# A hybrid RWKV-7 layer on one core: all SBUF buffers begin at the same remainder modulo 256 bytes

## The chip, the core and the metric

The kernel runs on one core of one Trainium2 chip. The metric is the device time of one execution in microseconds; lower is better. Everything is float32; most matrix products read their operands as float32r.

## The reference

One decoder layer (DEPTH 1) on x [1, 2048, 1024]: RWKV-7 time mixing, then a gated MLP with a causal depthwise convolution of width 3, each followed by a residual and a LayerNorm.

```
xx = shift(x) - x;  xr, xw, xk, xv, xa, xg = (x + xx * mix[i] for i in range(6))
r, k, v = xr @ w_rkv[0], xk @ w_rkv[1], xv @ w_rkv[2]          # 1024 x 1024 each
decay, a, gate = three two-layer LoRAs (64, 64 and 160 wide)
for each token t and head (16 heads of 64):                    # the recurrence
    state = state * w_t + (state . -kk_t) (kk_t * a_t) + v_t k_t;  y_t = state . r_t
x = LayerNorm(alpha * x + ((head_norm(y) + bonus) * gate) @ w_o)
h = causal_conv3(x @ w_in) + b;  u, g = split(h)               # 1024 -> 5632
x = LayerNorm(alpha * x + (silu(g) * u) @ w_out)               # 2816 -> 1024
```

## The kernel before

The program has four phases. **Sweeps** (about 9 to 715 us): three passes over the tokens, for k, r and v in this order. A pass takes 8 groups of 256 tokens; a group makes two token tiles of 128 by two halves `h` of 512 columns, and each of these four has 24 matmuls into one PSUM tile `ps`. **The recurrence** (to about 1280 us): 16 tiles of 128 tokens, in chunks of 64, by many small float32 products. **The output projection** (`z`, to about 1490 us). **The gated MLP** (to about 2965 us): four blocks of 512 tokens; in each, 22 chunks of 128 hidden units make two runs of 24 matmuls into `ps` (8 slices of the contraction, three products each) and, one chunk behind, 12 matmuls into the output accumulators `acc` for the first 512 columns. After the chunks the second 512 columns follow, all `acc`.

Every float32 product of these kinds is made of three float32r products (`mm3`, lines 139 to 143): both operands are split into a high and a low part by ACT and DVE, and TensorE multiplies high by high, low by high and high by low. So each of these matmuls loads its own 128x128 weights and then streams 512 columns. In the rows of the trace a matmul reads `out<-moving,weights`: `ps<-xH,wiH` streams xH over the weights wiH.

The order of the instructions is made by `Plan`, a list scheduler with a duration and a priority for each group. It reads nothing of addresses, and each engine then runs its list in order.

SBUF tiles come from pools (`tc.tile_pool`). A pool has a number of slots for each tag; a stack of pools grows upward from the left end of memory (`side="left"`), another downward from the right end (`side="right"`). The first tile on the left is `ident`, 512 bytes of each partition at address 16512; the right end is address 229344. Sizes that are no multiple of 256 bytes (`hb` with 514 floats, `xT` with 8 x 257, the small statistics tiles) move all that lies beyond them.

Of the kernel before, what the change touches and what calls it, by code (L numbers as in the profile page):

```python
# [11 lines left out]
F32 = mybir.dt.float32  # L12
# [5 lines left out]
PSUM = bass.MemoryType.PSUM  # L18
DRAM = bass.MemoryType.DRAM
# [11 lines left out]
def bc_rows(ap, n=128):  # L31
    """A DRAM row [1, n] read by every partition."""
    return bass.AP(tensor=ap.tensor, offset=ap.offset, ap=[[0, n], [1, ap.shape[-1]]])

# [5 lines left out]
class Plan:  # L40
    """Issue order of a set of instruction groups: each group runs on one engine, may take slots of a pool when it
    starts and give slots back when it ends; engines take the most urgent group that is ready. With fifo (or for
    the pools in it), the groups take the slots of a pool in the order in which they were added."""
# [74 lines left out]
class K:  # L118
# [3 lines left out]

    def ld(self, out, in_):
        return self.nc.sync.dma_start(out, in_)

    st = ld
# [7 lines left out]
    def split(self, H, L, x):  # L134
        """x = H + L exactly enough for float32: each part carries 12 bits."""
        self.nc.scalar.activation(H, x, AF.Copy)
        self.nc.vector.tensor_tensor(L, x, H, op=OP.subtract)
# [7 lines left out]
    def rsqrt(self, pool, out, x, n, m=None):  # L145
        """out = x ** -0.5 elementwise, [128, n], by Newton from a bit guess."""
        nc = self.nc
        w = pool.tile([128, n], F32, name="rsw", bufs=1)[:, 0:m or n]
        y = pool.tile([128, n], F32, name="rsy", bufs=1)[:, 0:m or n]
        nc.vector.tensor_scalar(w.bitcast(I32), x.bitcast(I32), 1, None, op0=OP.arith_shift_right)  # L150
        nc.vector.tensor_scalar(y.bitcast(I32), w.bitcast(I32), -1.0, float(0x5F3759DF), op0=OP.mult, op1=OP.add)
        for i in range(3):
            nc.vector.tensor_tensor(w, y, y, op=OP.mult)
            nc.vector.scalar_tensor_tensor(w, w, -0.5, x, op0=OP.mult, op1=OP.mult)
            nc.vector.scalar_tensor_tensor(out if i == 2 else y, w, 1.5, y, op0=OP.add, op1=OP.mult)

    # ------------------------------------------------------------------ run
    def run(self, phases="ASWF", scratch=None):
        tc, nc, a = self.tc, self.nc, self.a
        with ExitStack() as ctx:  # L160
# [3 lines left out]
            for t in range(NT):  # L164
                for q in ("vc", "Y"):
                    self.S[q, t] = mk([128, D], f"{q}_{t}")
                self.S["gs", t] = mk([128, 2, D], f"gs_{t}")
                for h in range(2):
                    # row t + 1 holds token t, but for the key, which is one row ahead, with the first token's last too
                    s = mk([129, 5, 512], f"in_{t}_{h}")  # L170
                    self.S["in", t, h] = s[1:129]
                    for i, q in enumerate(("r", "kp", "kkn", "b", "th")):
                        self.S[q, t, h] = s[0:128, i] if q == "kkn" else s[1:129, i]
                    self.S["kk0", t, h] = s[128:129, 2]
                    c = slice(h * 512, h * 512 + 512)
                    for q in ("vc", "Y"):
                        self.S[q, t, h] = self.S[q, t][:, c]
                    self.S["gateg", t, h] = self.S["gs", t][:, 0, c]
                    self.S["svbg", t, h] = self.S["gs", t][:, 1, c]
# [5 lines left out]
            self.ident = top.tile([128, 128], F32, name="ident")  # L185
# [17 lines left out]
    # -------------------------------------------------- projections, LoRAs  # L203
# [3 lines left out]
    def a_nodes(self, ctx, pl):  # L207
        """Adds the groups; returns those which end with part of the memory free, and all of it."""
# [4 lines left out]
        E = lambda **kw: st2.enter_context(tc.tile_pool(reuse_waits="tile", **kw))  # L213
# [7 lines left out]
        # what the recurrence's first tile can have before the end  # L221
        E = lambda **kw: st1.enter_context(tc.tile_pool(reuse_waits="tile", side="right", **kw))
# [41 lines left out]
        for sw, (q, wi, mm, ml) in enumerate((("k", 1, 2, 4), ("r", 0, 0, 1), ("v", 2, 3, 5))):  # L264
# [13 lines left out]
            def two(prio, ref, n_ld, d, fH, fL, deps=(), take=()):  # L278
                """ACT then DVE on a staged tile"""
                n1 = pl.add("ACT", 0.52 * d, prio, fH, [n_ld] + list(deps), take=take)  # L280
                return pl.add("DVE", 0.6 * d, prio, fL, [n1], give=("stg",))

            # first layer of the LoRA
# [27 lines left out]
            # the projection  # L311
# [16 lines left out]
            # what starts first: the first sweep with the projection, the others with the LoRA  # L328
# [7 lines left out]
            # second layer of the LoRA  # L336
# [59 lines left out]
            users = []  # L396
# [4 lines left out]
            def front(g):  # L401
# [4 lines left out]
                # the very first products go by parts of the contraction, and before the LoRA's  # L406
# [54 lines left out]
                # hidden units of the LoRA  # L461
                pn = prep("l", ml, wt + o["l0"] if start else gb + o["ml"], ("xT",) if start else ())

                def f_l1(X=X, sw=sw, q=q):
                    """The hidden units of the LoRA, in two parts that are added later."""
                    hp = X["hp"] = ph.tile([128, 256], F32, name="hp")
                    A = C["l1A", sw]
                    for k in range(KD):
# [4 lines left out]
                        else:  # L473
                            # the even and the odd parts in the two halves of the columns
# [57 lines left out]
            # the first halves of the last groups come before the second ones, for the next sweep's weights  # L532
# [196 lines left out]
    # ------------------------------------------------------ the recurrence  # L729
# [4 lines left out]
    def s_nodes(self, ctx, pl, n_1, n_2, w, f):  # L734
        """Adds the groups; n_1 frees part of the memory, n_2 all of it."""
# [3 lines left out]
        Q = {}  # L739
# [10 lines left out]
        def f_open1():  # L750
            """On the right, what W and the FFN have first at the top."""
            nonlocal inv, wkp, ldp, pw, xui, triI, gmask, cols, gm4, nbI, nbIn, nbE, scE
            E = lambda st=pools1, **kw: st.enter_context(tc.tile_pool(reuse_waits="tile", side="right", **kw))
# [13 lines left out]
            # one head's rows of a pair, zeros in the other's: the products use all rows of the array  # L767
# [3 lines left out]
        def f_open2():  # L771
            nonlocal cst, wk, ch2, sm, pm, pc
            E = lambda st=pools2, **kw: st.enter_context(tc.tile_pool(reuse_waits="tile", side="left", **kw))
# [39 lines left out]
        for t in range(NT):  # L813
# [4 lines left out]
            for h in range(2):  # L818
# [54 lines left out]
                for i, n_x in ((0, n_M), (1, n_R)):  # L873
# [7 lines left out]
                    def f_ar(t=t, h=h, i=i):  # L881
# [3 lines left out]
                        else:  # L885
                            # row t holds the key of the token after it, the last row that of the first
# [50 lines left out]
            # the inverses  # L937
# [45 lines left out]
            for c in range(2):  # L983
# [11 lines left out]
                # the block above them  # L995
# [35 lines left out]
                def f_ga(t=t, c=c):  # L1031
                    # A_ab has been read: its columns take the decayed keys, next to A_ak
                    for e in range(2):
                        CP(V[t]["Gm"][es(e), e, c, :, 0:64], V[t]["AR"][es(e), c, :, 0])
# [7 lines left out]
            # the chunks in turn  # L1042
# [7 lines left out]
            # a chunk's step; that of the last tiles in halves of the heads, which follow one another closely  # L1050
# [94 lines left out]
        # products into a spare bank where the engine would fall to its slow clock  # L1145
# [13 lines left out]
    # ------------------------------------ output projection, first LayerNorm  # L1159
# [4 lines left out]
    def w_nodes(self, ctx, pl, n_first, n_ch1, xds, Q, n_rest, stores, f):  # L1164
        """Adds the groups to the recurrence's plan; n_first frees part of its memory, n_ch1 the pool ch1 in Q, n_rest the rest."""
# [11 lines left out]
        def f_open(early):  # L1177
            E = lambda st=ctx, **kw: st.enter_context(
                tc.tile_pool(reuse_waits="tile", side="right" if early else "left", **kw))
# [16 lines left out]
        def f_ch1():  # L1196
            """What the first two tiles need before the recurrence ends."""
# [18 lines left out]
        def weights(h, k):  # L1216
            i = 8 * h + k

            def f_ld():
                # the high and low parts take what the recurrence has left  # L1220
# [45 lines left out]
        def rsqrt(t, u, pr, deps):  # L1266
            """One rsqrt: the heads' norms of tile t, the LayerNorm's of tile u."""
# [32 lines left out]
        def bank(kind, early):  # L1300
            """The PSUM banks in turn, the early ones alone before the recurrence ends."""
# [56 lines left out]
        for t in range(NT):  # L1358
# [4 lines left out]
            for h in range(2):  # L1363
                e = bank("pz", t < 1)
                if t < 2:
                    # in small groups, as the weights come, between the recurrence's last
# [54 lines left out]
    # --------------------------------------------------- gated MLP with conv  # L1421
# [3 lines left out]
    def f_nodes(self, ctx, pl, Q, n_early, n_w, n_rest, zs, gn, n_sx, n_x1):  # L1425
        """Adds the groups to the plan; n_early, n_w and n_rest free more and more memory."""
# [18 lines left out]
        def f_mid():  # L1445
            E = lambda **kw: ctx.enter_context(tc.tile_pool(reuse_waits="tile", side="right", **kw))
# [4 lines left out]
        def f_rest():  # L1451
            E = lambda **kw: ctx.enter_context(tc.tile_pool(reuse_waits="tile", side="left", **kw))
# [27 lines left out]
        xfree = []          # the last users of the x tiles of the block before  # L1480
        for B in range(NB):
# [29 lines left out]
            # the banks of the first products and of the outputs' first half change places from block to block  # L1511
# [10 lines left out]
            def wout(f, h, pr, mm=True, acc_mm=acc_mm, abank=abank, an=an, accs=accs):  # L1522
                """One chunk's part of the outputs; returns the last groups of the token tiles, or the weights."""
# [111 lines left out]
            def add(h, tl, n, pr, XR=XR, accs=accs, LN=LN, xrn=xrn, abank=abank):  # L1635
                """The residual and the statistics of half a row."""
# [49 lines left out]
            # the last chunks' weights stay, and the token tiles end one after another  # L1686
# [96 lines left out]
```

## Time and profile before

| | |
|---|---|
| runs, us | 2981.27, 2984.16, 2985.99 (median 2984.16) |
| span of the profiled execution, us | 2981.2 |
| TensorE matmul busy, share | 2845.6 us, 95% |
| VectorE busy, share | 2084.5 us, 70% |
| ScalarE busy, share | 1740.4 us, 58% |
| DMA packets, bytes | 298555, 424.08 MB |

The profiled execution's own time is its span: 2981.2 us, 3.0 us under the median of the runs. Matmuls overlap their neighbours in the trace, so the mean length of one in a row (some 396 ns) is not its share of the time. What one costs is the distance from its start to the start of the next: the start of the first of a run is taken from the start of what follows the run, and divided by the count.

### The profile page before, as it was taken

Reading aid. Unit: us, or ns where it says so; the run is one execution under the profiler, and the core shown is the slowest. Engines: PE = TensorE matmul, PEld = TensorE weight load, DVE = VectorE, ACT = ScalarE, POOL = GpSimd, SP = SyncE. Lnnn points to the kernel's source line nnn. Section 1 sums busy time; section 2 is a strip of 40 time slices with the busy share of each in tenths; the row PEclk is TensorE's granted clock in tenths of the full one; section 3 lists DMA queues with packets and bytes.
Section 4 is the critical chain, followed back from the end, with each engine's and each line's share of the span. In section 5 each row is a group of like instructions: output and inputs, shape, how many; then the busy total and the mean of one; then the engine's idle time right before and its main releaser. Section 6 shows DMA issues by size and latency. Waiting matters only on the chain.

```text
span 2981.2 us, 51766 instructions
## 1 busy us (share of the span) xinstructions
PE 2845.6 (95%) x19392; PEld 2321.1 (78%) x19392; DVE 2084.5 (70%) x4288; ACT 1740.4 (58%) x4668; POOL 53.6 (2%) x96
## 2 busy tenths in 40 slices
PE   7999999998799999799999999999999999999997
PEld 5776778887677777678888887888888888888886
DVE  7888768986899999779765555474554745547454
ACT  8888557664578788878454444444444444444441
POOL 0000000001000000001100000000000000000000
PEclk9999999999899999799999999999999999999999
DMA  6346555435455565568552223242232422324222
GB/s 202 143 167 222 175 183 191 152 114 175 129 149 161 153 164 160 133 220 315 179 178 94 92 97 120 93 154 97 89 127 96 148 98 85 133 95 153 90 87 78
DMA packets 298555, 424.08 MB, mean 142 GB/s; under 512 B 153952, under 2 KB 179552, under 8 KB 294208
## 3 DMA queue, kind: packets, MB, share of 16 engines
q1 hardware_dynamic: 286976, 379.87, 39.5%
q0 software_dynamic: 11328, 40.90, 3.8%
q8 instruction: 153, 2.51, 0.4%
q14 instruction: 98, 0.80, 0.1%
HBM read 311.57 MB, written 109.12 MB: 141 GB/s over the span
## 4 chain that ended last, share of the span: by engine, by line
issue 56%; PE 20%; DVE 12%; ACT 8%; DMA 3%; POOL 1%; SPq 0%; POOLq 0%; ACTq 0%; DVEq 0%
PE ps L141 4%; PE ps L142 4%; PE ps L143 4%; DVE BKn L904 3%; ACT junk L619 3%; PE G L744 2%; DVE itmp L966 1%; DVE XU L971 1%; DVE Gm L931 1%; PE Y L744 1%; DMA l<-in 1%; ACT junk L1260 1%; PE csI L744 1%; ACT UV L743 1%; PE tb L912 1%
## 5 line engine op out<-in xcount | busy, mean ns | idle before, releaser
L143 PE MATMUL ps<-xH,wiL 128*128 128x512 f32 x1408 | 557.9, 396 | 0.5 <-DVE wiL L1571 0.3
L1571 DVE TENSOR_TENSOR wiL<-wis,wiH 128x1024 fp32r<-128x1024 f32 x176 | 215.4, 1224 | 488.5 <-ACT wiH L1432 488.5
L141 PE MATMUL ps<-xH,wiH 128*128 128x512 f32 x1408 | 556.9, 396 | 0.0
L142 PE MATMUL ps<-xL,wiH 128*128 128x512 f32 x1408 | 556.8, 395 | 0.0
L1432 ACT ACTIVATE hb<-ps 128x512 f32<-128x512 f32 x176 | 105.3, 598 | 518.9 <-PE ps L143 518.8
L141 PE MATMUL ps<-WH,xiH 128*128 128x512 f32 x768 | 307.5, 400 | 14.6 <-ACT xiH L231 9.1
L143 PEld LDWEIGHTS ps<-xH,wiL 128*128 128x128 f32 x1408 | 264.5, 188 | 65.6 <-DVE wiL L1571 2.1
L142 PEld LDWEIGHTS ps<-xL,wiH 128*128 128x128 f32 x1408 | 264.4, 188 | 63.7
L141 PEld LDWEIGHTS ps<-xH,wiH 128*128 128x128 f32 x1408 | 264.5, 188 | 62.9
L142 PE MATMUL ps<-WL,xiH 128*128 128x512 f32 x768 | 305.1, 397 | 2.0 <-DVE WL L326 2.0
L143 PE MATMUL ps<-WH,xiL 128*128 128x512 f32 x768 | 304.4, 396 | 0.0
L1599 DVE SCALAR_TENSOR_TENSOR cv<-hb,cw,cv 128x512 f32<-128x512 f32 x352 | 263.4, 748 | 20.7 <-ACT cv L1595 14.5
L142 PE MATMUL acc<-woL,aH 128*128 128x512 f32 x688 | 269.3, 391 | 1.5 <-DVE woL L1536 1.5
L143 PE MATMUL acc<-woH,aL 128*128 128x512 f32 x688 | 269.9, 392 | 0.0
L141 PE MATMUL acc<-woH,aH 128*128 128x512 f32 x688 | 268.5, 390 | 0.0
L1432 ACT ACTIVATE wiH<-wis 128x1024 fp32r<-128x1024 f32 x178 | 188.8, 1061 | 5.8 <-DMA wis<-in_w_in_dram 5.8
L141 PEld LDWEIGHTS ps<-WH,xiH 128*128 128x128 f32 x768 | 146.3, 190 | 54.4 <-ACT xiH L231 9.1
L1432 ACT ACTIVATE woH<-wos 128x512 fp32r<-128x512 f32 x172 | 108.7, 633 | 114.4 <-PE acc L143 110.1
L142 PEld LDWEIGHTS ps<-WL,xiH 128*128 128x128 f32 x768 | 146.5, 191 | 34.6 <-DVE WL L326 2.5
L143 PEld LDWEIGHTS ps<-WH,xiL 128*128 128x128 f32 x768 | 146.3, 190 | 33.5 <-DVE xiL L450 0.2
L142 PEld LDWEIGHTS acc<-woL,aH 128*128 128x128 f32 x688 | 129.2, 188 | 32.4 <-DVE woL L1536 3.1
L141 PEld LDWEIGHTS acc<-woH,aH 128*128 128x128 f32 x688 | 129.2, 188 | 29.1 <-ACT woH L1432 0.5
(243 smaller groups left out, 5351.8 us busy)
## 6 DMA issues: line engine op xcount, KB each, us to landing
wis<-in_w_in_dram SPq DMA_DIRECT2D x176, 512.0 KB
wos<-in_w_out_dram SPq DMA_DIRECT2D x172, 256.0 KB
l<-in SPq DMA_DIRECT2D x32, 1280.0 KB
xT<-in_xT_dram SPq DMA_DIRECT2D x21, 1028.0 KB
in<-kp SPq DMA_DIRECT2D x64, 256.0 KB
stg<-in_w_rkv_dram SPq DMA_DIRECT2D x48, 256.0 KB
gs<-gs SPq DMA_DIRECT2D x24, 512.0 KB
in<-kr SPq DMA_DIRECT2D x32, 256.0 KB
```

The source lines that it names most:

```text
L141: nc.tensor.matmul(ps, lH, rH, start=start, stop=False)
L142: nc.tensor.matmul(ps, lH, rL, start=False, stop=False)
L143: nc.tensor.matmul(ps, lL, rH, start=False, stop=stop)
L619: nc.scalar.activation(junk, Z["kr"][:, 64 * i:64 * i + 64], AF.Square, accum_out=st["ss"][:, tl, i:i + 1])
L743: CP = lambda out, in_, **kw: nc.scalar.activation(out, in_, AF.Copy, **kw)
L744: MM = lambda out, l, r, **kw: nc.tensor.matmul(out, l, r, **{**dict(start=True, stop=True), **kw}, skip_group_check=True)
L904: TT(dst[rows, :, e], pe8(l[:, 1 if part else 3], e), pe8(V[t]["Pi", h], e), op=OP.mult)
L912: nc.tensor.transpose(ps[:, p], V[t]["BKn"][:, c, hd:hd + 2].rearrange("q e i -> q (e i)"), self.ident)
L931: TT(V[t]["Gm"][:, e, c, 4 * h:4 * h + 4], V[t]["G", h, c, e], gm4, op=OP.mult)
L1432: CP = lambda out, in_, **kw: nc.scalar.activation(out, in_, AF.Copy, **kw)
L1571: TT(W["L"], W["s"], W["H"], op=OP.subtract)
L1599: STT(R[j], W["hb"][:, i:i + 512], C["cw"][:, fc, i:i + 1], R[j], op0=OP.mult, op1=OP.add)
```

## The change: one remainder for all SBUF buffers

SBUF pools are wrapped in `Pool256`. Its `tile` pads the free size of a tile so that all slots of a tag together take a multiple of 256 bytes; what the kernel then uses is the unpadded part. `ident` is padded by 24 floats at its front (608 bytes in place of 512), which moves the left stack from remainder 128 to 224, the remainder of the right end. PSUM and DRAM pools stay as they were.

```
+class Pool256:
+    def tile(self, shape, dtype, bufs=None, **kw):
+        b = bufs or self.bufs
+        n = math.prod(shape[1:])
+        u = 64 // math.gcd(64, 16 * b) * 16 if n % 64 else 64
+        if n % u == 0 or n % 64 == 0:
+            return self.pool.tile(shape, dtype, bufs=b, **kw)
+        x = self.pool.tile([shape[0], -(-n // u) * u], dtype, bufs=b, **kw)[:, 0:n]
...
+    def pool(self, st, **kw):
+        p = st.enter_context(self.tc.tile_pool(**kw))
+        return p if kw.get("space") is not None else Pool256(p, kw["bufs"])
...
-            self.ident = top.tile([128, 128], F32, name="ident")
+            self.ident = top.tile([128, 152], F32, name="ident")[:, 24:152]
...
-        E = lambda **kw: st2.enter_context(tc.tile_pool(reuse_waits="tile", **kw))
+        E = lambda **kw: self.pool(st2, reuse_waits="tile", **kw)
```

The last edit is made for each stack of pools. The diff also drops comments and docstrings, which moves line numbers and makes no instruction. Every engine has the same instructions in the same order as before, on the same slots; a few waits of the first sweep on GpSimd's memsets are held by a neighbouring instruction. What differs is the addresses. The remainder modulo 256 at which the operands of the large products begin, in the two built programs (slices into a tile go by multiples of 512 bytes):

| product (moving, weights) | matmuls | before | after |
|---|---|---|---|
| MLP `ps` (xH or xL, wiH or wiL) | 4224 | 128, 160 | 224, 224 |
| MLP `acc`, chunks 0 to 9 (woH or woL, aH or aL) | 960 | 224, 224 | 224, 224 |
| MLP `acc`, chunks 10 to 21 (48 more, of other tiles, went from 160, 160) | 1104 | 224, 160 | 224, 224 |
| sweeps `ps`, first half h=0 (WH or WL, xiH or xiL) | 1152 | 224, 0 | 224, 224 |
| sweeps `ps`, second half h=1 | 1152 | 0, 0 | 224, 224 |
| `z` (wo, woH or woL, with yH or yL) | 672 | 160, 160 | 224, 224 |
| `z` (the same, with yE of the first two tiles) | 96 | 160, 128 | 224, 224 |

The tiles from which the sweeps store (`kp`, `kr`, `w`, `av`) go from remainder 0 to 224, `Gm` and `XT` of the recurrence from 128 to 224, the staged weights `wis` from 160 to 224, `wos` mostly stays at 224.

## Rows read from the trace of the kernel before

**Rows 1.** The page: busy us, share of the span and instructions of each engine.

```profile
PE 2845.6 (95%) x19392; PEld 2321.1 (78%) x19392; DVE 2084.5 (70%) x4288; ACT 1740.4 (58%) x4668; POOL 53.6 (2%) x96
```

**Rows 2.** Busy time by stretch: k sweep, r and v sweeps, recurrence, MLP twice.

```profile
core 0: us, PE busy (x) PEld busy (x) DVE busy (x) ACT busy (x) POOL busy (x), PEclk, DMA share, GB/s
20.00:300.00 280.00, 257.05 (x1132) 195.10 (x1131) 236.16 (x516) 244.51 (x893) 0.12 (x1) 0.95 0.52 178
300.00:600.00 300.00, 300.00 (x1438) 245.26 (x1437) 242.56 (x481) 198.82 (x652) 0.11 (x1) 1.00 0.51 173
780.00:1200.00 420.00, 380.66 (x7163) 325.10 (x7161) 397.86 (x1276) 330.14 (x668) 6.39 (x12) 0.99 0.57 154
1500.00:1800.00 300.00, 300.00 (x1297) 242.60 (x1296) 166.15 (x203) 148.50 (x292) 0.86 (x1) 1.00 0.32 111
2500.00:2900.00 400.00, 399.67 (x1724) 323.23 (x1723) 223.40 (x292) 178.88 (x342) 2.13 (x4) 1.00 0.32 109
```

**Rows 3.** What TensorE waited for in the MLP, 1490 to 2970 us (all rows listed: us, times, longest).

```profile
PE acc L142 <- DVE woL L1536: 1.5, 3, 0.8
PE ps L143 <- DVE wiL L1571: 0.3, 2, 0.2
```

**Rows 4.** The same in the k sweep, 20 to 300 us: the longest two.

```profile
PE p L581 <- ACT av L601: 9.4, 7, 2.6
PE hp L476 <- DVE hz L496: 3.5, 1, 3.5
```

**Rows 5.** The page's groups: counts of the large products, one line of three each.

```profile
L141 PE MATMUL ps<-xH,wiH 128*128 128x512 f32 x1408 | 556.9, 396 | 0.0
...
L141 PE MATMUL ps<-WH,xiH 128*128 128x512 f32 x768 | 307.5, 400 | 14.6 <-ACT xiH L231 9.1
```

**Rows 6.** TensorE's timeline in the MLP: firsts of acc, ps, acc, ps (start us, us).

```profile
2301.14 0.39 PE L141 MATMUL acc<-woH,aH 128*128 128x512 f32 x1
...
2303.89 0.40 PE L141 MATMUL ps<-xH,wiH 128*128 128x512 f32 x1
...
2309.49 0.39 PE L141 MATMUL acc<-woH,aH 128*128 128x512 f32 x1
```

**Rows 7.** The same, 36 matmuls of acc on end, chunks 0 to 2.

```profile
2164.50 0.40 PE L141 MATMUL acc<-woH,aH 128*128 128x512 f32 x1
...
2172.68 0.39 PE L141 MATMUL acc<-woH,aH 128*128 128x512 f32 x1
```

**Rows 8.** TensorE's timeline in the r sweep: 24 of the first half.

```profile
388.60 0.40 PE L141 MATMUL ps<-WH,xiH 128*128 128x512 f32 x1
...
394.21 0.39 PE L581 MATMUL p<-l2A,gH 128*128 128x512 f32 x1
```

**Rows 9.** The same group, 24 of the second half.

```profile
408.72 0.39 PE L141 MATMUL ps<-WH,xiH 128*128 128x512 f32 x1
...
414.16 0.39 PE L581 MATMUL p<-l2A,gH 128*128 128x512 f32 x1
```

**Rows 10.** DVE groups, shapes apart: 1500 to 1627 us, then 1657 to 1795 us.

```profile
L1615 DVE TENSOR_TENSOR aL<-cv,aH 128x512 fp32r<-128x512 f32 x9 | 6.2, 691 | 7.6 <-ACT aH L1432 7.6
...
L1615 DVE TENSOR_TENSOR aL<-cv,aH 128x512 fp32r<-128x512 f32 x10 | 6.9, 692 | 7.0 <-ACT aH L1432 7.0
```

**Rows 11.** DMA issues of GpSimd's queue: KB each, median us from issue to landing.

```profile
out_dram<-xr POOLq DMA_DIRECT2D x16, 512.0 KB, 4.1
...
vc<-kr POOLq DMA_DIRECT2D x4, 256.0 KB, 3.7
gs<-w POOLq DMA_DIRECT2D x4, 256.0 KB, 2.8
```

**Rows 12.** The recurrence, 780 to 1200 us: TensorE's only listed wait for a DMA.

```profile
PE csI L744 <- DMA l<-in: 1.3, 3, 0.6
```

More of the change, by code (lines that the diff above doesn't have):

```diff
@@ L33, in bc_rows, with __init__ @@
     return bass.AP(tensor=ap.tensor, offset=ap.offset, ap=[[0, n], [1, ap.shape[-1]]])
+class Pool256:
+    def __init__(self, pool, bufs):
+        self.pool, self.bufs = pool, bufs
+    def tile(self, shape, dtype, bufs=None, **kw):
[5 more added lines that the diff above has]
+        x = self.pool.tile([shape[0], -(-n // u) * u], dtype, bufs=b, **kw)[:, 0:n]
+        if len(shape) > 2:
+            d = " ".join(f"d{i}" for i in range(1, len(shape)))
+            x = x.rearrange(f"p ({d}) -> p {d}", **{f"d{i}": shape[i] for i in range(2, len(shape))})
+        return x
 class Node:
@@ L220, in a_nodes @@
         plp = E(name="a_pl", bufs=sl["pl"], space=PSUM)
-        E = lambda **kw: st1.enter_context(tc.tile_pool(reuse_waits="tile", side="right", **kw))
+        E = lambda **kw: self.pool(st1, reuse_waits="tile", side="right", **kw)
         lp1 = E(name="a_l1", bufs=1)
@@ L752, in f_open1 @@
             nonlocal inv, wkp, ldp, pw, xui, triI, gmask, cols, gm4, nbI, nbIn, nbE, scE
-            E = lambda st=pools1, **kw: st.enter_context(tc.tile_pool(reuse_waits="tile", side="right", **kw))
+            E = lambda st=pools1, **kw: self.pool(st, reuse_waits="tile", side="right", **kw)
             if w:
@@ L772, in f_open2 @@
             nonlocal cst, wk, ch2, sm, pm, pc
-            E = lambda st=pools2, **kw: st.enter_context(tc.tile_pool(reuse_waits="tile", side="left", **kw))
+            E = lambda st=pools2, **kw: self.pool(st, reuse_waits="tile", side="left", **kw)
             chs[1] = Q["ch1"] = E(stL, name="s_ch1", bufs=1)
@@ L1177, in f_open @@
         def f_open(early):
-            E = lambda st=ctx, **kw: st.enter_context(
-                tc.tile_pool(reuse_waits="tile", side="right" if early else "left", **kw))
+            E = lambda st=ctx, **kw: self.pool(st, reuse_waits="tile", side="right" if early else "left", **kw)
             if early:
@@ L1445, in f_mid @@
         def f_mid():
-            E = lambda **kw: ctx.enter_context(tc.tile_pool(reuse_waits="tile", side="right", **kw))
+            E = lambda **kw: self.pool(ctx, reuse_waits="tile", side="right", **kw)
             Q["wk"] = E(name="f_wk", bufs=2)
@@ L1451, in f_rest @@
         def f_rest():
-            E = lambda **kw: ctx.enter_context(tc.tile_pool(reuse_waits="tile", side="left", **kw))
+            E = lambda **kw: self.pool(ctx, reuse_waits="tile", side="left", **kw)
             Q["fr"] = E(name="f_r", bufs=1)
```

## The prediction

> **What bounds the kernel now.** I read the page first: TensorE has matmuls in flight for 95% of the span, VectorE is busy for 70%, ScalarE for 58% [rows 1]. A share over four phases says little, so I read the table of stretches next [rows 2]. [...] What TensorE waited for there comes to 1.8 us in almost 1,500 [rows 3]. So the MLP, half of the kernel, lasts as long as its matmuls take to follow one another. The r and v sweeps are the same (300.00 of 300.00 us). The k sweep is not: 257 of 280 us, with 23 us of gaps, most of them waits for ACT and DVE [rows 2, 4]. In the recurrence VectorE is busy for 397.86 of 420 us, and what TensorE gains is lost in waiting for it [rows 2].
>
> In the stretches that TensorE fills, then, only one number counts: the distance from one matmul's start to the next. The timeline gives it by product. In the MLP a run of 24 first products starts at 2303.89 us and the outputs after it at 2309.49: 5.60 us, **233.3 ns** each. The 12 outputs before it, from 2301.14, take 2.75 us, **229.2 ns** each [rows 6]. A run of 36 outputs of chunks 0 to 2 takes 8.18 us, **227.2 ns** each [rows 7]. In the r sweep 24 products of the first half take 5.61 us, **233.8 ns** each [rows 8], 24 of the second half of the same group, 20 us later, 5.44 us, **226.7 ns** each [rows 9]. All of these have the same shape, the same type, the same clock and no wait between them.
>
> The table of remainders in the section on the change orders them. First products: streamed tile at 128, weights at 160, 233.3 ns. First half of the sweep: 224 and 0, 233.8 ns. Second half: 0 and 0, 226.7 ns. Outputs, chunks 0 to 2: 224 and 224, 227.2 ns. Outputs, chunks 10 on: 224 and 160, 229.2 ns. Modulo 64 the five pairs are (0, 32), (32, 0), (0, 0), (32, 32), (32, 32): **where the two operands of TensorE differ by 32 modulo 64 a matmul takes some 233.5 ns; where they agree, 227 to 229.** Neither operand's own remainder decides, since each of the two occurs on both sides. I can't say from the trace why, only that a weight load runs under each matmul, so that both operands are read at a time.
>
> **The change, part by part.** It makes no instruction, moves none and adds no byte to a transfer. What it changes is five addresses modulo 256, and by the table every large product then has its operands at 224 and 224.
>
> *MLP, first products.* There are 3 x 1408 = 4224 [rows 5]. From 233.3 ns they should come to what agreeing operands take. The nearest rows are those with fully equal remainders, 226.7 and 227.2 ns [rows 7, 9]; I take 227.5, a little above both, since 229.2 occurs too [rows 6]. 5.8 ns x 4224 = 24.5 us. Bounds: 233.3 - 229.2 = 4.1 ns, 17.3 us; 233.3 - 226.7 = 6.6 ns, 27.9 us. All of it lies on the path, since nothing else fills this phase: VectorE and ScalarE have 45% and 50% of room, and the weights are wanted 2% sooner from DMA queues that are busy for a third. [...]
>
> *Sweeps, first halves.* Half of 3 x 768 = 2304 matmuls [rows 5], in 48 runs of 24. 5.61 - 5.44 us is 0.17 us for a run; I take 0.16, as the new state should lie at 227.2 rather than at 226.7. 48 x 0.16 = 7.7 us, a third in each sweep. In r and v it counts in full, 5.1 us. In the k sweep ACT and DVE are late at many places, and a TensorE that is ready sooner waits longer; I count half, 1.3 us. Sum 6.4 us. Bounds: r and v alone at the smaller step of 4.1 ns, 768 x 4.1 ns = 3.1 us; everything at 0.17 us, 8.2 us.
>
> *MLP, outputs of chunks 10 to 21.* 1104 matmuls go from 64 apart to equal. 229.2 against 227.2 ns [rows 6, 7] would be 2.2 us; the difference between agreeing pairs may have other causes, so I count 1.0 us, with bounds 0 and 2.2.
>
> *Second halves of the sweeps, outputs of chunks 0 to 9, z.* They agree before and after: nothing. 96 products of z with yE differed, in a phase in which TensorE waits: nothing, at most 0.6 us.
>
> *VectorE and ScalarE.* aL is made from aH at 224 in chunks 0 to 9 and from aH at 160 later, and takes 691 and 692 ns [rows 10]. I take nothing for them; at 1 ns for each of some 9,000 instructions it would be 9 us, but spread over engines that are late only in the k sweep and the recurrence, so at most 2 us either way on the path.
>
> *The recurrence.* Small float32 products, whose operands mostly agreed already, on a chain that VectorE sets. Nothing, 2 us either way.
>
> *DMA.* The stores of the sweeps leave remainder 0, the 128-byte pieces of Gm and XT now straddle a multiple of 256 in half of the cases. In the trace 256 KB from remainder 0 land in 2.8 and 3.7 us, 512 KB from remainder 160 in 4.1 us [rows 11]: for its bytes the tile that began off a multiple of 256 was no slower. I count nothing.
>
> Sum: 24.5 + 6.4 + 1.0 = 31.9 us, say 31, with bounds of 17.3 + 3.1 - 2 = 18 and 27.9 + 8.2 + 2.2 + 2 = 40. The profiled execution would go from 2981.2 to 2950 us. The median of the runs lies 3.0 us above its span, so for the runs: 2984.2 - 31 = **2953 us**, between 2944 and 2966.
>
> **The rivals.**
>
> *No difference: the remainder is not the cause.* The runs that I compared differ in their tiles too, and in what ACT, DVE and the DMA engines do beside them. Then 233.3 ns stays and the time is 2984 us. For it: the trace has no two runs that differ by an address alone. Against it: the pair in the sweep comes from one group, 20 us apart, and both (0, 32) and (32, 0) are slow while (0, 0) and (32, 32) are fast. That the padding doesn't bring what it says would end here too, but the addresses in the built program are as in the table. Chance 5%.
>
> *A smaller gain.* The weights tiles of the first products are rewritten by ACT and DVE for every 24 matmuls, while TensorE reads their neighbours; in the sweeps the weights stay for a whole group. Agreement may bring less in the MLP. Half of the step: 2.9 ns x 4224 = 12.2 us, and 3 us of the sweeps: 2969 us. For it: agreeing pairs do spread, from 226.7 to 229.2 ns. Chance 6%.
>
> *Slower: transfers that straddle.* If a packet from or to a row at 224 cost so much more that the DMA engines become the bound, it would be in the recurrence, which has the smallest pieces and the fullest queues, 0.57 of the engines' time [rows 2]. The point from which it decides is 1 / 0.57, packets 1.75 times as long. At twice the time the queues would need 1.14 of it, 14% of the 565 us from 715 to 1280, so 79 us; with the 31 us gained, 2984 + 48 = 3032 us. For it: no row shows a piece of 128 bytes that straddles. Against it: TensorE waits for a DMA for 1.3 us of these 420 [rows 12], and rows 11. Chance 3%. [...]
>
> **How the numbers follow.** Forecast 86%, the smaller gain 6%, no difference 5%, slower 3%. The predicted time is that of the forecast, 2953 us. The range is 2944 to 2966 us: the bounds of the sum, and what it leaves out, 14%, are the rivals. A measurement of this kernel can tell about 0.2%, 6 us, from no change. Faster by more than that: forecast and smaller gain, 92%. Within it: 5%. Slower: 3%.
>
> **What would show it.** In the profile after: a run of 24 first products in the MLP in 5.44 to 5.50 us, not 5.60; 24 products of a sweep's first half in 5.44 to 5.47 us, as its second half; outputs of the late chunks at 2.72 to 2.75 us for 12; the busy time of matmuls on the page some 30 us less; VectorE's and ScalarE's as before; the gaps of the k sweep a little longer; the recurrence as long as before within 2 us. The prediction is wrong if those 24 stay at 5.60 us with the operands at 224 and 224 (then the remainder is no cause), or if they fall and the MLP doesn't get shorter (then something else bounds it, and its wait would stand in the list of waits in place of the 1.8 us).

## The result, and the profile after

The changed kernel takes **2950.7 us** (median of four runs, 2945.05 to 2954.42) against 2984.4 us for the kernel before beside it: a ratio of **0.988, interval 0.986 to 0.990**. The forecast was 2953 us in a range of 2944 to 2966. In two later comparisons the same kernel took 2951.50 and 2946.93 us. Its profiled execution has a span of 2943.1 us, 7.6 us under the median of the runs that it came with, so its difference to the span of before, 38.1 us, is a few us more than the runs show (33.6).

The page of the kernel after, which answers to [rows 1]: busy us, share of the span and instructions of each engine.

```profile
PE 2803.2 (95%) x19392; PEld 2317.1 (79%) x19392; DVE 2086.2 (71%) x4288; ACT 1742.4 (59%) x4668; POOL 53.7 (2%) x96
```

The instructions are the same, the matmuls' busy time is 42.4 us less, VectorE's and ScalarE's stand within 2 us. The same five stretches as in [rows 2], in the kernel after (columns as there):

```profile
20.00:300.00 280.00, 256.16 (x1142) 196.47 (x1141) 236.79 (x516) 245.76 (x897) 0.12 (x1) 0.96 0.53 180
300.00:600.00 300.00, 300.00 (x1455) 248.16 (x1454) 246.74 (x488) 201.32 (x665) 0.11 (x1) 1.00 0.52 175
780.00:1200.00 420.00, 378.83 (x7157) 323.18 (x7157) 398.26 (x1279) 331.70 (x671) 6.41 (x12) 1.00 0.58 151
1500.00:1800.00 300.00, 299.25 (x1322) 247.14 (x1321) 174.85 (x217) 150.70 (x292) 0.86 (x1) 1.00 0.36 118
2500.00:2900.00 400.00, 398.32 (x1753) 328.36 (x1752) 226.48 (x299) 175.81 (x333) 2.13 (x4) 1.00 0.34 111
```

The clock is as before, 1.00 in the MLP. In 300 us of the MLP TensorE now starts 1322 matmuls where it started 1297, in 300 us of the r and v sweeps 1455 for 1438. What it waited for in the MLP (us, times, longest), as [rows 3]:

```profile
PE acc L165 <- DVE woL L1559: 2.2, 4, 0.8
PE ps L166 <- DVE wiL L1594: 0.5, 3, 0.2
```

2.7 us in 1447 in place of 1.8 in 1480: nothing has come up to take the place of what went. TensorE's timeline of the kernel after, in the MLP: firsts of an acc, a ps and an acc run, as [rows 6].

```profile
2259.89 0.39 PE L164 MATMUL acc<-woH,aH 128*128 128x512 f32 x1
...
2262.61 0.39 PE L164 MATMUL ps<-xH,wiH 128*128 128x512 f32 x1
...
2268.05 0.39 PE L164 MATMUL acc<-woH,aH 128*128 128x512 f32 x1
```

And in the r sweep, the very run of 24 of [rows 8]:

```profile
386.09 0.39 PE L164 MATMUL ps<-WH,xiH 128*128 128x512 f32 x1
...
391.53 0.39 PE L605 MATMUL p<-l2A,gH 128*128 128x512 f32 x1
```

12 outputs in 2.72 us and 24 first products in 5.44, both **226.7 ns** each; the 24 of the sweep in 5.44 us, 226.7 ns, where they took 5.61. By phase (us): sweeps, z and MLP begin with the start of their first large product, the recurrence with the start of the last `ps<-WH,xiH`, and the MLP ends with the start of its last output:

| kernel | sweeps | recurrence | z | MLP | span |
|---|---|---|---|---|---|
| before | 705.5 | 564.6 | 211.4 | 1474.0 | 2981.2 |
| after | 699.1 | 566.8 | 208.2 | 1442.8 | 2943.1 |
| after, second profile (e8) | 699.7 | 566.4 | 210.5 | 1444.9 | 2948.3 |
| after, third profile (e9) | 699.9 | 566.5 | 209.0 | 1442.7 | 2944.6 |

### The profile page after: what moved, and what is told of

Its sections match the earlier page's. It is cut to its first block, busy times and chain, and to the rows that moved or that the text cites. A ratio compares the mean times of both kernels' runs of the same rounds, so it can differ in the third digit from the quotient of the medians.

```text
span 2943.1 us, 51765 instructions
## 1 busy us (share of the span) xinstructions
PE 2803.2 (95%) x19392; PEld 2317.1 (79%) x19392; DVE 2086.2 (71%) x4288; ACT 1742.4 (59%) x4668; POOL 53.7 (2%) x96
## 4 chain that ended last, share of the span: by engine, by line
issue 55%; PE 21%; DVE 12%; ACT 7%; DMA 3%; POOL 1%; SPq 0%; POOLq 0%; ACTq 0%; DVEq 0%
PE ps L164 4%; PE ps L165 4%; PE ps L166 4%; DVE BKn L928 3%; ACT junk L643 2%; PE G L768 2%; DVE XU L995 2%; DVE itmp L990 2%; DVE Gm L955 1%; DMA l<-in 1%; PE Y L768 1%; DMA in<-av 1%; DVE l L879 1%; ACT junk L1283 1%; DVE l L875 1%
## 5 line engine op out<-in xcount | busy, mean ns | idle before, releaser
L166 PE MATMUL ps<-xH,wiL 128*128 128x512 f32 x1408 | 548.2, 389 | 0.5 <-DVE wiL L1594 0.5
L164 PE MATMUL ps<-xH,wiH 128*128 128x512 f32 x1408 | 548.1, 389 | 0.0
L165 PE MATMUL ps<-xL,wiH 128*128 128x512 f32 x1408 | 547.8, 389 | 0.0
L166 PEld LDWEIGHTS ps<-WH,xiL 128*128 128x128 f32 x768 | 146.2, 190 | 31.2 <-DVE xiL L474 0.2
```

Source lines behind the costliest of these rows:

```text
L164: nc.tensor.matmul(ps, lH, rH, start=start, stop=False)
L165: nc.tensor.matmul(ps, lH, rL, start=False, stop=False)
L166: nc.tensor.matmul(ps, lL, rH, start=False, stop=stop)
```

## The experiments

Below, **distance** is the remainder of the weights minus that of the streamed tile, modulo 256. In the kernel before it is 32 in the MLP's ps and the sweeps' first halves, 192 in the late outputs, 0 in the rest; z with yE has 224.

**e2: the first products alone.** On the kernel before, wiH and wiL are moved from 160 to 128, the remainder of xH and xL (`off_tile` makes a tile 256 bytes longer and uses it from an offset).

```
-  W["H"], W["L"] = (Q["wi"].tile([128, KD, 128], F32R, ...) for x in "HL")
+  W["H"], W["L"] = (off_tile(Q["wi"], [128, KD, 128], F32R, 56, ...) for x in "HL")
```

> The kernel before, with the weights tiles wiH and wiL alone moved by 224 bytes, from remainder 160 to 128, that of xH and xL; nothing else moves within its tile. Theory: 24 first products in 5.44 to 5.46 us in place of 5.60, so 24 to 28 us less for 4224 of them, and up to 2 us more from outputs of chunks 0 to 9: 2954 to 2960 us, 0.990 to 0.992 of before. Rival (the remainder is not the cause): 2984 us.

Measured: 2964.38 us, ratio 0.994 (0.992 to 0.995), MLP 1454.2 us. So the remainder alone does it, but the MLP gained 19.8 us where 24 to 28 were expected. TensorE's timeline in e2 tells why: the start of a ps run, its tenth matmul, and the acc that follows the run.

```profile
1537.93 0.39 PE L149 MATMUL ps<-xH,wiH 128*128 128x512 f32 x1
...
1540.01 0.39 PE L149 MATMUL ps<-xH,wiH 128*128 128x512 f32 x1
...
1543.41 0.40 PE L149 MATMUL acc<-woH,aH 128*128 128x512 f32 x1
```

The first 9 take 2.08 us, 231 ns each, the other 15 take 3.40 us, 226.7 ns. In e2 ps has both operands at 128 and acc has its stream at 224, so TensorE goes from one remainder to the other at each acc run, and in 131 of the 176 ps runs it is the tenth matmul from which the interval stays at 225 to 228 ns. The kernel before has the same in its equal pairs: of the 36 outputs of [rows 7], from 2164.50 to 2172.68, the ninth starts here:

```profile
2166.33 0.39 PE L143 MATMUL acc<-woH,aL 128*128 128x512 f32 x1
```

8 in 1.83 us, 229 ns each, then 28 in 6.35 us, 226.8 ns. The 227.2 ns of rows 7 was a mean of the two.

**e3: the left stack at 192.** On the kernel after, ident is padded by 16 floats and not 24; where the weights lie on the left and the streamed tile on the right the distance is then 224, and operands on one side stay equal.

```
-  self.ident = top.tile([128, 152], F32, name="ident")[:, 24:152]
+  self.ident = top.tile([128, 144], F32, name="ident")[:, 16:144]
```

> The changed kernel, with ident padded by 16 floats in place of 24: the whole left stack begins at remainder 192, the right one stays at 224. The MLP's first products (both operands on the left) and the outputs of chunks 0 to 9 (both on the right) still agree; the outputs of chunks 10 to 21 (aH, aL on the left) and the first halves of the sweeps (WH, WL on the right) are 32 apart. Theory: 1104 outputs go from 226.7 to 233 ns, 7 us, the sweeps give back their 6 us: 13 us more than the changed kernel, 2960 to 2967 us. Rival 1 (any remainder will do): as the changed kernel, 2951 us. Rival 2 (one kind of product out of step slows all that stand beside it): up to 2984 us.

Measured: 2969.01 us, 0.995 (0.993 to 0.996). Late outputs 233.6 ns, the sweeps' first halves 233.2; ps, equal at 192, 227.8 on average, with some three to seven slower ones behind each acc run. MLP 1456.7 us, 13.9 over the kernel after: with the sizes padded but the two stacks 32 apart, about half of the gain is gone. The time lies 2 us over the range expected: that range left out the slower starts of equal pairs, 1.05 ns x 4224 = 4.4 us in ps and 2.2 ns x 960 = 2.1 us in the early outputs.

**e4: other engines' tiles.** On the kernel after, `cv` (ACT and DVE) and `wos` (DMA, ACT, DVE) are moved by 32 bytes.

```
-  Q["wk"].tile([128, 512], F32, name=f"cv{j}", bufs=sl[f"c{j}"])
+  off_tile(Q["wk"], [128, 512], F32, 8, name=f"cv{j}", bufs=sl[f"c{j}"])
```

> The changed kernel, with tiles that TensorE doesn't read moved by 32 bytes: cv (VectorE and ScalarE, each chunk) and wos (DMA, ScalarE and VectorE). Theory (only TensorE's own two operands count): first products and outputs stay at 226.7 ns, MLP 1443 us, 2945 to 2955 us. Rival (tiles of the other engines count too, and the MLP is fast because all of them agree): the MLP goes back towards 1474 us.

Measured, in a single run: 2948.54 us, ps and acc 226.7 ns, MLP 1441.5 us, as in the kernel after. The tiles that only other engines and the DMA read and write may begin elsewhere, at least by 32 bytes.

**e1 and e5: the distance.** On the kernel before, wiH and wiL get an offset that goes with the chunk.

```
+WOFF = [o // 4 for o in (224, 0, 32, 64, 96, 128, 160, 192, 228, 232, 236, 240, 244, 248, 252, 8, 16, 24, 40, 208, 48, 112)]
-  def f_H(W=W):
-      W["H"], W["L"] = (Q["wi"].tile([128, KD, 128], F32R, ...) for x in "HL")
+  def f_H(W=W, fc=fc):
+      W["H"], W["L"] = (off_tile(Q["wi"], [128, KD, 128], F32R, WOFF[fc % NF], ...) for x in "HL")
```

The edit shown is that of e5. In e1 the first line of `f_H` was left as it was, without `fc=fc`, so that every chunk took the last offset: all ran at distance 144, and e1 is no scan.

> The kernel before, with one thing changed: the weights tiles wiH and wiL of the MLP's first products are padded by 256 bytes and begin, from chunk to chunk, at 22 different distances from the streamed tiles xH and xL (0, 32, 64 ... 224 bytes, and 4 to 28, 40, 48, 56, 72, 80, 144, 240), both runs of 24 of a chunk at the same one. Theory (the two operands of TensorE decide, modulo 64): the second run of 24 takes 226.5 to 229 ns a matmul at 0, 64, 128 and 192, some 233 ns at 32, 96, 160 and 224, and at distances between 32 and 64 something between. Rival 1 (the remainder is not the cause): 233.3 ns at all 22. Rival 2 (only an equal remainder modulo 256 helps): 227 ns at 0 alone.

Measured in e1, a single run: 2959.66 us, MLP 1453.3. Two neighbouring runs of 24 in e1, each with the acc that follows it:

```profile
1512.21 0.40 PE L152 MATMUL ps<-xH,wiH 128*128 128x512 f32 x1
...
1517.67 0.40 PE L152 MATMUL acc<-woH,aH 128*128 128x512 f32 x1
...
1518.37 0.39 PE L152 MATMUL ps<-xH,wiH 128*128 128x512 f32 x1
...
1523.96 0.39 PE L152 MATMUL acc<-woH,aH 128*128 128x512 f32 x1
```

5.46 us and 5.59 us, 227.5 and 232.9 ns each, at the same addresses modulo 256, with nothing between them but three outputs. The two read different slots of the weights, 4352 bytes apart in the built program. The fourth run after the second of them has both operands and the PSUM bank at its very addresses:

```profile
1547.36 0.40 PE L152 MATMUL ps<-xH,wiH 128*128 128x512 f32 x1
...
1552.82 0.40 PE L152 MATMUL acc<-woH,aH 128*128 128x512 f32 x1
```

5.46 us, 227.5 ns. So what came before decides too. Of e1's 176 half-chunks (runs of 24) 165 settled at 227 and 11 at 233: six of the first eight, and the five whose second matmul is followed by a gap, 303 to 1430 ns from its start to the next. At distance 0 in e5 three runs have such a gap, of 520 to 557 ns, and all three came back to 226.7.

> The kernel before, with the weights of the first products (wiH, wiL) at an offset that goes with the chunk: 22 distances from the streamed tile (which stays at 128), 192 matmuls at each. Read is the interval from start to start in the second 24 of the 48 matmuls that a chunk has at one distance, so that what follows a change of the remainder is over. Theory A, what counts is the distance modulo 64, in steps of 32: distances 32, 96, 160, 224 give 233 ns; 0 and 128 give 226.7; 64 and 192 give 227 to 229; multiples of 4 and 16 in between lie with 0, near 227, as the one distance of 144 did. Theory B, what counts is how far apart the two lie within 64 bytes: a smooth slope, 4 to 12 bytes at 227 to 229, 16 at 230, 24 and 28 near 233, 40 falling again. Theory C, only 0 is fast: everything else lies at 229 or above. The time as a whole says little, about 2965 us under A, 2970 under B or C.

Measured in e5, a single run: 2979.55 us. TensorE's timeline in e5, first ps of a run and the acc behind it: 24 at distance 128, then 48 at 192, 48 at 240.

```profile
1542.09 0.39 PE L152 MATMUL ps<-xH,wiH 128*128 128x512 f32 x1
...
1547.66 0.39 PE L152 MATMUL acc<-woH,aH 128*128 128x512 f32 x1
...
1572.68 0.39 PE L152 MATMUL ps<-xH,wiH 128*128 128x512 f32 x1
...
1583.68 0.40 PE L152 MATMUL acc<-woH,aH 128*128 128x512 f32 x1
...
1753.22 0.39 PE L152 MATMUL ps<-xH,wiH 128*128 128x512 f32 x1
...
1764.11 0.39 PE L152 MATMUL acc<-woH,aH 128*128 128x512 f32 x1
```

5.57 us for 24, 232.1 ns; 11.00 for 48, 229.2; 10.89 for 48, 226.9. All distances, as the mean interval in each of 8 half-chunks behind its first nine matmuls and without its last (good to some 0.3 ns):

| distance | ns | distance | ns |
|---|---|---|---|
| 0 | 226.6 to 227.7 | 48, 56, 64, 72 | 233.3 to 233.5 |
| 4 | 232.4 | 80 | 231.8 to 232.0 |
| 8 | 230.7 to 230.8 | 96 | 234.3 |
| 12 | 230.0 to 230.3 | 128 | 232.4 |
| 16, 20 | 233.2 to 233.4 | 144 | 233.1 to 233.4 (e1: 226.6 or 233) |
| 24 | 230.0 to 231.4 | 160 | 233.4 to 233.5 |
| 28 | 226.6 three times, 235.1 five | 192 | 228.9 five times, 233.4 three |
| 32 | 233.0 to 233.4 | 224 | 233.3 to 233.5 |
| 40 | 226.7 twice, 233 to 233.5 six | 240 | 226.6 to 226.7 |

None of the three theories holds. The intervals of a run settle into a cycle that repeats to its end (226.7 each; 236 and 231 in turn; 229, 232, 226). Distance 0 came to 226.7 each time. At 28, 40, 144 and 192 operands at the same addresses (the PSUM bank differs in e5) settled at 227 to 229 in one run and at 233 or more in another. Distance 240 was at 226.7 in all its eight. No cycle had a mean under 226.6.

**e12: 64 apart.** The clearest test of the prediction's rule: on the kernel before, wiH and wiL alone go from 160 to 192.

```
-  W["H"], W["L"] = (Q["wi"].tile([128, KD, 128], F32R, ...) for x in "HL")
+  W["H"], W["L"] = (off_tile(Q["wi"], [128, KD, 128], F32R, 8, ...) for x in "HL")
```

> The kernel before, with wiH and wiL alone moved by 32 bytes, from 160 to 192: 64 from the streamed tile at 128, where they were 32 from it. By the prediction's rule (only 32 modulo 64 is slow) the first products take 227 to 229.2 ns, 17 to 27 us are gained, 2957 to 2967 us. By what the scan of distances showed (only wholly equal remainders settle at 226.7 from any start; 64 apart repeats 231 and 236) they take 233 to 234 ns and nothing is gained: 2981 to 2988 us.

Measured: 2985.83 us, ratio 1.000 (0.999 to 1.001). 48 ps and the acc behind them in e12:

```profile
1562.88 0.39 PE L149 MATMUL ps<-xH,wiH 128*128 128x512 f32 x1
...
1574.08 0.39 PE L149 MATMUL acc<-woH,aH 128*128 128x512 f32 x1
```

11.20 us, 233.3 ns each. The rule "only 32 modulo 64 is slow" gave 17 to 27 us for this edit; the edit gains nothing.

**e7: the left stack at 160.** On the kernel after, ident is padded by 8 floats; operands on two sides then have distance 192.

```
-  self.ident = top.tile([128, 152], F32, name="ident")[:, 24:152]
+  self.ident = top.tile([128, 136], F32, name="ident")[:, 8:136]
```

> The kernel after, with ident padded by 8 floats in place of 24: the left stack begins at 160, the right one stays at 224. Late outputs (1104), the sweeps' first halves (1152) and most of z (720) then have operands 64 apart; the first products have 160 and 160, early outputs 224 and 224. Theory A, 64 apart costs 2 ns and not 6, and a change of the remainder from one run of products to the next costs some matmuls after it: late outputs and first halves 229 ns, first products 227.3 to 228, together 7 to 11 us over after, 2957 to 2963. Rival, remainders must be wholly equal (as 192 and 224, 18 us over after): 2966 to 2970. Rival, only 32 modulo 64 costs anything, and there is nothing behind a change of the remainder: within 2 us of after.

Measured: 2961.30 us, 0.991 (0.9895 to 0.9926); the kernel after in the same comparison 2951.50. Late outputs 230.3 ns, first halves 229.8, ps (equal, at 160) 227.8 and early outputs (equal, at 224) 229.1: the equal ones lose 1.1 and 2.4 ns, in the first matmuls of a run, up to ten, where the run before lies at another remainder.

**e6 and e8 to e11: does the common value matter?** e6 and e10 have both stacks at 128 (ident unpadded, 24 floats at the right end), e11 at 192 (16 floats left, 8 right); e8 and e9 are the kernel after itself. The edit of e6, on the kernel after:

```
+  topr = ctx.enter_context(tc.tile_pool(name="topr", bufs=1, side="right"))
+  topr.tile([128, 24], F32, name="padr")
-  self.ident = top.tile([128, 152], F32, name="ident")[:, 24:152]
+  self.ident = top.tile([128, 128], F32, name="ident")
```

> The kernel after, with both stacks moved from 224 to 128, by ident at the left end as it was before and 96 bytes at the right end. Theory A, it is the equality of the operands' remainders that counts and not its value: large products at 226.7 ns as after, MLP 1442 to 1444 us, total as after within 3 us (2948 to 2954). If the recurrence's 2 us more in after came from 128-byte pieces of Gm and XT that straddle a multiple of 256, they end here: 565 us in place of 566.8, and the total 2 us under after. Rival, 224 is a good value in itself: the MLP's first products rise above 228 ns, total 2957 us or more.

> The kernel after, unchanged, beside the others of this call: 2945 to 2955 us, ratio 0.987 to 0.990. A second profile tells how much of the phases' differences is spread: the MLP within 1 us of 1442.8, the sweeps within 1 us of 699.1 in sum. If the 2.2 us that the recurrence took longer were caused by the addresses, it is 566 to 567 us again; if it was spread, it lies anywhere from 564 to 567.

Measured, side by side: 2946.38 us at 128 (0.986, 0.985 to 0.988), 2951.50 at 224 (0.988, 0.986 to 0.990). Large products of MLP 226.7 ns in both. The recurrence took 565.0 at 128 and 566.4 at 224. That left 5 us open, so they were compared again, with 192 beside them.

> The kernel after, unchanged, in more rounds, as the measure for the next two: 2947 to 2953 us, ratio 0.987 to 0.990.

> Both stacks at 128, in more rounds. If the common value doesn't matter, it is within 2 us of the kernel after in this call. If pieces of 128 bytes that straddle a multiple of 256 (Gm and XT, where the remainder is 224) cost the recurrence some 2 us, it is 2 to 5 us under the kernel after, with a recurrence of 564.5 to 565.5 us and not 566 to 567.

> Both stacks at 192 (ident padded by 16 floats at the left end, 32 bytes at the right end). Pieces of 128 bytes at 192 straddle a multiple of 256 as at 224. If straddling is what separates 128 from 224, the recurrence takes 566 to 567 us and the total is that of the kernel after within 2 us; if it was spread, 128 and 192 differ by no more than 224 and either. Large products 226.7 ns in any case.

Measured: 2946.93 us at 224, 2947.77 at 128, 2947.49 at 192, each with a ratio of 0.987 (0.9855 to 0.9884 or 0.9885). The 5 us are gone: as far as the time can tell, it doesn't matter which of these three values it is. By phase one thing is left: the sweeps took 701.6 and 703.7 us in the two profiles at 128, against 699.1 to 700.0 in four at 224 (the three above and e4) and 699.9 at 192. No run shows whether that is the value or spread. The recurrence, 566.5, 565.4 and 566.3 us, agrees with straddling pieces that cost about 1 us, but e2 and e12, which differ in the MLP's weights alone, had 564.4 and 569.1 there, so 1 us of it can't be put down to anything.

## Why the prediction came out, and where its rule was wrong

*What bounds the kernel.* Right. TensorE waits for 1.8 us in the MLP before and 2.7 us after, and the MLP followed the interval from start to start.

*First products, 24.5 us.* Mechanism right, size a little low. They came to 226.7 ns, not to 227.5: 6.6 ns x 4224 = 27.9 us, the upper bound. I had put 0.8 ns on top because 229.2 occurs among the "agreeing" pairs. Those 229 ns belong to pairs at distance 192 and to the first matmuls behind a change of the remainder, neither of which is left when everything lies at 224.

*Sweeps, 6.4 us.* Measured 6.4: the r sweep 2.2 and the v sweep 2.5 us shorter (2.6 predicted for each), the k sweep 1.65 (1.3 predicted; 1.0 and 1.3 in e8 and e9). The k sweep's part is not shown: before's profile has 240.2 us there, but the four others with before's sweeps (e1, e2, e5, e12) 239.0 to 239.3, and the kernel after 238.6 to 239.2 in its three. Of the exact agreement a part is luck.

*Late outputs, 1.0 us.* They went from 228.9 to 226.7 ns on average: 2.2 ns x 1104 = 2.4 us. Half of the step was taken because its cause was open; it was the remainder.

*Early outputs, 0.* The one zero that failed. They had equal operands before and yet took 228.4 ns on average, since they follow a ps run at another remainder, and take 226.7 now: 1.6 ns x 960 = 1.5 us. With the two above this makes 31.8 us for the MLP, which fell by 31.2 (29.0 and 31.3 in the other two profiles); 25.5 were predicted.

*The total.* MLP and sweeps together lost 37.6 us by the first pair of profiles, where 31.9 were added up and 31 taken. The runs show 33.6, and 35.0 and 38.8 in the two later comparisons. So the forecast is right in its parts but low in most of them, and that it came within 2.3 us of the median is in part luck.

*z, recurrence, VectorE, ScalarE: 0.* z was 3.2 us shorter and the recurrence 2.2 longer in the first pair of profiles. z takes 208.2 to 210.5 us in three profiles of the kernel after, and 208.5 to 211.4 in five kernels that have before's z (before, e1, e2, e5, e12): spread. The recurrence is named above; 2.2, 1.8 and 1.9 us longer in three profiles is about the 2 us that were allowed.

*DMA: 0.* The line of the hardware queue (packets, MB, share of 16 engines' time in the span), before:

```profile
q1 hardware_dynamic: 286976, 379.87, 39.5%
```

after:

```profile
q1 hardware_dynamic: 286976, 379.87, 41.3%
```

and with both stacks at 128 (e10):

```profile
q1 hardware_dynamic: 286976, 379.87, 40.7%
```

The span alone, 1.3% shorter, would make 40.0% of 39.5. Most of the rest is spread: e1, e2, e5 and e12, whose layout is before's but for the MLP's weights, have 40.0 to 40.7%. One difference stays, in the recurrence. Its 98304 packets of 128 bytes took 12.7 to 12.8 ns on average in before and those four and 12.3 in the two profiles at 128, where the pieces of Gm and XT don't straddle; 13.5 in the three at 224 and 13.3 at 192, where half of them do. All of its packets together took 317 to 321 and 315 us (sum over the 16 engines, divided by 16), and 327 to 329 and 324. So straddling may cost 4 to 10% of such a packet, not all of it shown, since before and 128 differ without it. But the queues had room: 224, 128 and 192 take the same time. The rival of straddling transfers needed packets 75% longer and reckoned with twice the time. No run shows that factor: the packets of 128 bytes took 13.5 ns on average after and 12.7 before, 6% more.

*The rule.* "Where the two operands differ by 32 modulo 64 a matmul takes some 233.5 ns; where they agree, 227 to 229" is wrong in its second half: 64 and 128 apart take 233.3 and 232.4 ns (e12, e5). The large products of before had only the distances 0, 32, 192 and 224, and I folded 192 into 0 because both looked fast. The forecast held since the change makes the distance 0 everywhere, of the distances that the rule calls fast the only one that settled at 226.7 in every run; on a change that left the weights 64 apart it would have failed, as e12 shows.

*The rivals.* "No difference" falls with e2, which moves one pair of tiles and nothing else. "A smaller gain" was thought of as the rewriting of the weights; e2 did gain less, 19.8 us and not 27.9, through the change of the remainder between runs, which a common remainder takes away. Moving the weights alone took the interval from 233.3 to 226.7 ns (e2), so it depends on where the two begin relative to each other, wherever that arises.

*What stays open.* Why some distances settle in one of two cycles, and where the dependence between the two operands arises. The runs show that the addresses of both decide and, at some distances, history too; they don't show the place. Distances between those of the table, and offsets under 4 bytes, weren't tried.

## What to carry to other kernels

Where TensorE runs without gaps and each matmul loads its own weights (shown here for 128x512 float32r products), compare the interval from start to start between products of one shape: if it differs, look at where the two operands begin modulo 256. Put both, and the operands of all products that follow one another, at the same remainder: 128, 192 and 224 gave the same time, while 32, 64 and 128 bytes apart took 232 to 233 ns in place of 226.7. When a rule is drawn from a table, list which distances the table has before folding them.

## What the runs showed of the hardware

- 128x512 float32r matmuls, each with its own weights, follow one another at 226.7 ns at best, at a granted clock of 1.00 (the MLP of the kernel after). None of the 22 distances of e5 settled at less, within the 0.3 ns to which its means are good.
- Equal modulo 256 is enough: in the built program of the kernel after, the operands of ps are 256 apart modulo 512 and nearly all those of acc 0, and both take 226.7 ns, while 128 apart takes 232.4 (e5). Equal is not the only fast distance: 240 settled at 226.6 to 226.7 in all of its eight runs.
- The intervals settle into repeating cycles (in e5 226.7 ns each, or 236 and 231 in turn, or 229, 232, 226). At distance 144 two runs of e1 with both operands and the PSUM bank at the same addresses took 232.9 and 227.5 ns a matmul, so the addresses alone don't decide which cycle a run stays in. The eight runs of e5 at distance 0 all came back to 226.7, three of them after gaps of over 500 ns.
- With equal operands, a change of the common remainder from one run to the next (128 to 224 in e2) costs up to nine matmuls at 231 ns; in the kernel after, without a change, 167 of 176 ps runs are at 225 to 228 ns from their first matmul on.
- The recurrence's packets of 128 bytes took 13.5 ns on average where half of the pieces of Gm and XT straddle a multiple of 256 bytes (after, e8, e9), and 12.3 to 12.8 where none does (before, e6, e10); the kernel's time doesn't show it.
